# Where three groups of tiles lie in SBUF: the tiles of h 64 bytes apart in their distance from 2 KB, and two gaps in front of the weights and of m

## The chip, the cores and the metric

The kernel runs on one core of a Trainium2 chip. The metric is the device time of one launch, in microseconds (us). Three runs of the kernel before took 1065.42, 1065.43 and 1065.94 us, so the median is 1065.43 us.

## The reference, cut to what matters

The program is two layers of a decoder trunk on 512 tokens of width 1024 and a last RMSNorm. In each layer one wide projection of the normalised input feeds three token mixers (attention, a short convolution, a retention) and their gates; three branch projections are merged and one more projection goes back to the residual stream:

```python
h = rms_norm(x, norm_g)
proj = h @ w_in                       # (512, 1024) @ (1024, 8704)
...
merged = g[:, :, 0] * (branches[0] @ w_branch[0])
for i in range(1, N_BRANCH):
    merged = merged + g[:, :, i] * (branches[i] @ w_branch[i])
return x + (merged @ w_out).astype(x.dtype)
```

Nearly all arithmetic is in `h @ w_in`, `branches[i] @ w_branch[i]` and `merged @ w_out`.

## The kernel before, in words

Everything is laid out with channels on the 128 partitions and the 512 tokens along the free dimension, so one tile of 128x512 float32 takes 2 KB in each partition. Every product is made three times (`mm3`, lines 190 to 193): both operands are split into a high and a low part of type float32r, and line 191 multiplies high by high, line 192 high weights by the low part of the other operand, line 193 low weights by its high part. Each of the three is one matmul with its own load of 128x128 stationary values, which the profile lists as engine PEld.

The weights come as chunks of 128x1024 (4 KB per partition). `split_next` (line 207) copies a chunk's high part to `whi` on ScalarE (line 187) and takes the low part `wlo` on VectorE or GpSimd (line 184); three buffers of each turn. A stationary operand is 128 columns of such a chunk, so it starts at a multiple of 512 bytes from the chunk's start.

In each layer the value projections come first (`values`, line 367: the scaled input `xb` is stationary, the weights are moving). Then h is made, eight tiles with a high and a low part each, so 16 tiles of 2 KB (lines 411 to 417). `proj` (line 420) makes 128 output channels: a loop over k = 0 to 7, `mm3` with h tile k as the moving operand, 24 matmuls in all. There are 60 such projections in a layer. Between k = 3 and k = 4, and after k = 7, `tick` (line 241) may put a step of attention or retention into the stream: score products (line 466), transposes (line 592), value products (lines 191 to 193 on `st` and `vm`), or the two matmuls of a head's norm with the stationary `ones_p` (lines 499 and 500). `merge` (line 621) multiplies branch outputs (moving `xb`) by weights; `out_proj` (line 676) multiplies the merged tiles m (called `vm`, lines 639 to 641, moving) by weights, in the last layer in two halves of 256 tokens.

TensorE's order is written out by hand (line 350); the other engines' order is found by the scheduler when the program is built. Tiles get their addresses when the program is built, pool by pool and name by name in the order in which the names are first used. So all tiles of the large pool before start at the same distance from a multiple of 2 KB, since all sizes but the last are multiples of 2 KB: 384 bytes, for `xb`, `whi`, `wlo`, `qk`, `vm`, `h`, `st` and the rest. The small pool is packed in steps of 32 bytes; `ones_p`, a stationary operand, starts at byte 1440.

Of the kernel before, what the change touches and what calls it, by code (L numbers as in the profile page):

```python
# [18 lines left out]
P = 128  # L19
S = 512  # L20
# [134 lines left out]
def tile_hybrid_trunk(ctx: ExitStack, tc: tile.TileContext, xT, w, prm, lam, tab, cmat, outT):  # L155
# [12 lines left out]
    def t(tag, bufs, shape=(P, S), dt=F32):  # L168
        home = small if tag in SMALL else odd if tag == "wu" else sb
        return home.tile(list(shape), dt, tag=tag, bufs=bufs, name=tag)  # L170

    def tr(tag, bufs, shape=(P, S)):
        return t(tag, bufs, shape, F32R)

    def pj():
        return ps.tile([P, S], F32, tag="pj", bufs=NPJ, name="pj")
# [9 lines left out]
    def split(hi, lo, x, eng=V):  # L186
        A.copy(hi, x)  # L187
        lo_part(lo, x, hi, eng)
# [18 lines left out]
    def split_next():  # L207
        if not raws:
            prefetch()
        if raws:  # L210
            raw = raws.pop(0)
            hi, lo = tr("whi", 3, (P, 1024)), tr("wlo", 3, (P, 1024))
            for c in range(0, 1024, 512):
                c = slice(c, c + 512)
                if pos[0] or parts or c.start:
                    split(hi[:, c], lo[:, c], raw[:, c], G if c.start else V)
                else:
                    V.tensor_copy(hi[:, c], raw[:, c])
                    lo_part(lo[:, c], raw[:, c], hi[:, c])
            parts.append((hi, lo))  # L220
# [53 lines left out]
    nc.sync.dma_start(cm, cmat)  # L274
    ident, negmask, tri = (cm[:, i * P:(i + 1) * P] for i in range(3))
    ones_p = tr("ones_p", 1, (P, P))
    A.copy(ones_p, cm[:, 3 * P:4 * P])
    ones_d = t("ones_d", 1, (P, 1))
# [23 lines left out]

    H = [slice(0, 64), slice(64, 128)]
    klo = [tr("klo", 4) for _ in range(4)]
    for n, lo in enumerate(klo):
        G.memset(lo[H[1 - n % 2]].bitcast(F32), 0.0)
# [44 lines left out]
    for l in range(DEPTH):  # L351
# [59 lines left out]
        h = []  # L411
        for k in range(NK):
            hk = t("wa", 1)
            V.scalar_tensor_tensor(hk, x[k], ng[k], rrow, op0=ALU.mult, op1=ALU.mult)  # L414
            hi, lo = tr("h", 16), tr("h", 16)
            split(hi, lo, hk)
            h.append((hi, lo))
        rv = values_out(rbanks)
# [331 lines left out]
```

## Time and profile before

| | |
|---|---|
| median of three runs | 1065.43 us |
| the profiled execution itself | 1065.34 us |
| its span, first to last instruction | 1063.5 us |
| TensorE busy (PE) | 1053.9 us, 99% of the span |
| weight loads busy (PEld) | 881.7 us |
| VectorE, ScalarE, GpSimd busy | 681.9, 503.0, 318.7 us |
| mean granted TensorE clock | 0.998 of full speed |

The profile's page gives busy times, a picture of the span in slices, and the chain of work that ended last. A matmul's duration in it runs from its start to its modelled end; since matmuls are pipelined, the next one starts before that end, and what one matmul costs is the distance from its start to the next one's start, called spacing below. Starts are read from the timeline.

### The profile page before, as it was taken

The page shows a single profiled execution, that of the slowest core. Times are in us where ns is not written, and L with a number is a line of the kernel's source. Part 1 is how long each engine was busy: PE and PEld are TensorE (multiplying, and loading weights), DVE is VectorE, ACT ScalarE, POOL GpSimd, SP SyncE. Part 2 cuts the span into 40 slices and gives each one's busy share as a digit, 9 for nine tenths or more (in the row PEclk, how much of TensorE's full clock was granted, in tenths as well). Part 3 has the DMA queues.
Part 4 walks back from the last instruction along what each step waited for, and adds up shares of the span by engine and source line. Part 5 has one row for each costly group of instructions (what it writes and reads, how often), then busy time and mean ns, then how long its engine had stood idle before and what let it go on. Part 6 is the DMA issues. An engine that isn't in the chain of part 4 may idle for free.

```text
span 1063.5 us, 13847 instructions
## 1 busy us (share of the span) xinstructions
PE 1053.9 (99%) x5010; PEld 881.7 (83%) x5010; DVE 681.9 (64%) x1168; ACT 503.0 (47%) x943; POOL 318.7 (30%) x253
## 2 busy tenths in 40 slices
PE   9999999999999999999999999999999999999997
PEld 6888888888888888888888888888888888888896
DVE  8687686765677566345528876868556956654444
ACT  6454354543554554334434535445354645543353
POOL 6222232221233333232412212332123233333264
PEclk9999999999999999999999999999999999999999
DMA  6323222232234222444432232223213432133453
GB/s 258 106 93 100 88 71 96 83 119 85 74 119 139 77 85 78 128 129 149 149 99 83 87 109 80 80 84 119 96 60 100 139 100 80 61 107 129 128 190 119
DMA packets 34340, 113.64 MB, mean 107 GB/s; under 512 B 3936, under 2 KB 3936, under 8 KB 34272
## 3 DMA queue, kind: packets, MB, share of 16 engines
q1 hardware_dynamic: 34128, 112.50, 32.4%
q8 instruction: 39, 0.64, 0.3%
q14 instruction: 29, 0.24, 0.1%
q10 hardware_dynamic: 144, 0.26, 0.1%
HBM read 108.55 MB, written 4.19 MB: 106 GB/s over the span
## 4 chain that ended last, share of the span: by engine, by line
PE 93%; DVE 5%; ACT 1%; issue 1%; DMA 0%; SPq 0%; DVEq 0%; ACTq 0%
PE pj L191 28%; PE pj L192 28%; PE pj L193 28%; PE pa L466 3%; PE pa L192 1%; PE pa L193 1%; DVE wa L414 1%; PE pa L191 1%; DVE wlo L184 1%; PE pa L592 1%; DVE h L184 1%; DVE vm L382 1%; ACT h L187 1%; DVE xb L362 0%; PE pa L499 0%
## 5 line engine op out<-in xcount | busy, mean ns | idle before, releaser
L184 POOL TENSOR_TENSOR wlo<-wraw,whi 128x512 fp32r<-128x512 f32 x184 | 251.8, 1371 | 628.0 <-ACT whi L187 582.2
L191 PE MATMUL pj<-h,whi 128*128 128x512 f32 x960 | 379.4, 395 | 0.0
L192 PE MATMUL pj<-h,whi 128*128 128x512 f32 x960 | 374.7, 390 | 0.2
L193 PE MATMUL pj<-h,wlo 128*128 128x512 f32 x960 | 374.7, 390 | 0.0
L187 ACT CAST whi<-wraw 128x512 fp32r<-128x512 f32 x367 | 216.3, 617 | 220.9 <-PE pj L192 141.1
L184 DVE TENSOR_TENSOR wlo<-wraw,whi 128x512 fp32r<-128x512 f32 x184 | 153.1, 833 | 125.5 <-ACT whi L187 124.5
L193 PEld LDWEIGHTS pj<-h,wlo 128*128 128x128 f32 x960 | 180.2, 188 | 38.9 <-DVE wlo L184 0.3
L192 PEld LDWEIGHTS pj<-h,whi 128*128 128x128 f32 x960 | 180.5, 188 | 35.7 <-DVE h L184 1.1
L191 PEld LDWEIGHTS pj<-h,whi 128*128 128x128 f32 x960 | 180.4, 188 | 35.4
L191 PE MATMUL pj<-xb,whi 128*128 128x512 f32 x192 | 75.0, 391 | 0.0
L192 PE MATMUL pj<-xb,whi 128*128 128x512 f32 x192 | 74.9, 390 | 0.0
L193 PE MATMUL pj<-xb,wlo 128*128 128x512 f32 x192 | 74.7, 389 | 0.0
L579 ACT ACTIVATE p<-pa,nm 128x128 f32<-128x128 f32 (+3 forms) x64 | 33.5, 527 | 69.2 <-DVE nm L576 69.0
L503 DVE RECIPROCAL e<-e 128x512 f32<-128x512 f32 x16 | 53.6, 3351 | 18.0 <-ACT e L502 18.0
L187 ACT CAST st<-pa 128x256 fp32r<-128x256 f32 (+2 forms) x80 | 29.8, 373 | 70.5 <-DVE pa L521 40.5
L191 PE MATMUL pj<-vm,whi 128*128 128x256 f32 (+1 forms) x192 | 61.3, 319 | 0.0
L192 PE MATMUL pj<-vm,whi 128*128 128x256 f32 (+1 forms) x192 | 61.1, 318 | 0.0
L193 PE MATMUL pj<-vm,wlo 128*128 128x256 f32 (+1 forms) x192 | 61.1, 318 | 0.0
L636 DVE SCALAR_TENSOR_TENSOR wb<-wa,pj 128x512 f32<-128x512 f32 x32 | 22.0, 687 | 41.5 <-PE pj L193 38.3
L184 DVE TENSOR_TENSOR st<-pa,st 128x256 fp32r<-128x256 f32 (+2 forms) x80 | 33.6, 420 | 17.1 <-ACT st L187 16.5
L193 PEld LDWEIGHTS pj<-xb,wlo 128*128 128x128 f32 x192 | 36.0, 188 | 7.6
L191 PEld LDWEIGHTS pj<-xb,whi 128*128 128x128 f32 x192 | 36.1, 188 | 7.3
(132 smaller groups left out, 1433.6 us busy)
## 6 DMA issues: line engine op xcount, KB each, us to landing
wraw<-w SPq DMA_DIRECT2D x183, 512.0 KB, 3.4
tab<-tab SPq DMA_DIRECT2D x10, 512.0 KB, 3.4
xm<-xT SPq DMA_DIRECT2D x15, 256.0 KB, 3.7
xsave<-xm SPq DMA_DIRECT2D x8, 256.0 KB, 2.0
xm<-xsave SPq DMA_DIRECT2D x8, 256.0 KB, 2.6
outT<-p SPq DMA_DIRECT2D x8, 256.0 KB, 2.1
wraw<-w SPq DMA_DIRECT2D x2, 256.0 KB, 3.4
xm<-xT ACTq DMA_DIRECT2D x1, 256.0 KB, 3.0
```

The costliest lines, as they stand in the source:

```text
L184: eng.tensor_tensor(lo, x, hi, op=ALU.subtract)
L187: A.copy(hi, x)
L191: T.matmul(out, wh, xh, start=start, stop=False)
L192: T.matmul(out, wh, xl, start=False, stop=False)
L193: T.matmul(out, wl, xh, start=False, stop=stop)
L382: V.scalar_tensor_tensor(lo, banks[tt], rtok[:, tt:tt + 1], hi, op0=ALU.mult, op1=ALU.subtract)
L414: V.scalar_tensor_tensor(hk, x[k], ng[k], rrow, op0=ALU.mult, op1=ALU.mult)
L466: T.matmul(o, ac[i][:, asl], bc[i][:, bsl], start=i == 0, stop=i == 1)
L503: V.reciprocal(r, r)
L579: A.activation(pc[:, :n], sp[:, :n], AF.Exp, bias=nm, scale=0.125, accum_out=sm)
L592: T.transpose(tp[:, j * P:(j + 1) * P], p1[:, j * P:(j + 1) * P], ident)
L636: V.scalar_tensor_tensor(y, g, 1.0, o, op0=ALU.add, op1=ALU.mult)
```

## The change

The tag `h` with 16 rotating buffers becomes 16 tags `h0` to `h15` with one buffer each, high and low part of tile k being h(2k) and h(2k + 1). Each is allocated with 16 float32 more than are used, so 2112 bytes instead of 2048. A tile of 256 bytes per partition that nothing uses is allocated just before the first `whi`, one of 128 bytes just before the first `vm`.

```diff
     def tr(tag, bufs, shape=(P, S)):
+        if tag == "whi" and "gap0" not in gaps:
+            gaps["gap0"] = t("gap0", 1, (P, 64))
+        if tag == "vm" and "gap1" not in gaps:
+            gaps["gap1"] = t("gap1", 1, (P, 32))
         return t(tag, bufs, shape, F32R)
+
+    gaps = {}
...
-            hi, lo = tr("h", 16), tr("h", 16)
+
+            hi, lo = (tr(f"h{2 * k + i}", 1, (P, S + 16))[:, 0:S] for i in range(2))
             split(hi, lo, hk)
```

The built programs have the same instructions on all five engines in the same order, with the same waits; only names and addresses differ. The distance of a tile's start from a multiple of 2 KB, in bytes:

| tiles | before | after |
|---|---|---|
| `xm`, `wa`, `cm`, `klo`, `xb` | 384 | 384 |
| `whi`, `wlo`, `qk`, `e1`, `e2` | 384 | 640 |
| `vm` (values, later m) | 384 | 768 |
| `h`, by number n = 0 to 15 | 384 | 768 + 64 n |
| `tab`, `ez`, `p0`, `p1`, `st`, `sq`, `wc`, `wu` | 384 | 1792 |
| `ones_p` (small pool) | 1440 | 1440 |

## Rows read from the trace of the kernel before

**Rows 1.** The page: span, busy times, slices of PE and its clock, chain by engine.
```profile
span 1063.5 us, 13847 instructions
PE 1053.9 (99%) x5010; PEld 881.7 (83%) x5010; DVE 681.9 (64%) x1168; ACT 503.0 (47%) x943; POOL 318.7 (30%) x253
...
PEclk9999999999999999999999999999999999999999
...
PE 93%; DVE 5%; ACT 1%; issue 1%; DMA 0%; SPq 0%; DVEq 0%; ACTq 0%
```

**Rows 2.** Busy time by stretch: 100 to 1000 us (busy, count; PEclk, DMA share, GB/s).
```profile
100.00:1000.00 900.00, 899.88 (x4151) 749.12 (x4150) 575.02 (x992) 421.44 (x789) 253.34 (x192) 1.00 0.31 100
```

**Rows 3.** Matmuls grouped by line and shape: count, busy us, mean ns, idle before.
```profile
L191 PE MATMUL pj<-h,whi 128*128 128x512 f32 x960 | 379.4, 395 | 0.0
L192 PE MATMUL pj<-h,whi 128*128 128x512 f32 x960 | 374.7, 390 | 0.2
L193 PE MATMUL pj<-h,wlo 128*128 128x512 f32 x960 | 374.7, 390 | 0.0
L191 PE MATMUL pj<-xb,whi 128*128 128x512 f32 x192 | 75.0, 391 | 0.0
...
L191 PE MATMUL pj<-vm,whi 128*128 128x256 f32 x128 | 36.4, 284 | 0.0
...
L191 PE MATMUL pj<-whi,xb 128*128 128x512 f32 x64 | 25.5, 399 | 0.0
...
L191 PE MATMUL pa<-whi,xb 128*128 128x512 f32 x64 | 25.3, 396 | 0.0
...
L191 PE MATMUL pj<-vm,whi 128*128 128x512 f32 x64 | 24.9, 389 | 0.0
```

**Rows 4.** Timeline of TensorE, seven undisturbed projections (start us, duration us).
```profile
179.77 0.39 PE L191 MATMUL pj<-h,whi 128*128 128x512 f32 x1
...
217.85 0.22 PE L466 MATMUL pa<-qk 128*128 128x128 f32 x1
```

**Rows 5.** Timeline of TensorE, output projection with 256 columns, last layer.
```profile
1049.40 0.28 PE L191 MATMUL pj<-vm,whi 128*128 128x256 f32 x1
...
1053.72 0.28 PE L191 MATMUL pj<-vm,whi 128*128 128x256 f32 x1
```

**Rows 6.** Timeline of TensorE around a head's norm (lines 499, 500).
```profile
137.28 0.39 PE L192 MATMUL pj<-h,whi 128*128 128x512 f32 x1
...
138.18 0.40 PE L193 MATMUL pj<-h,wlo 128*128 128x512 f32 x1
138.42 0.39 PE L499 MATMUL pa<-st,ones_p 128*128 128x512 f32 x1
138.65 0.39 PE L500 MATMUL pa<-st,ones_p 128*128 128x512 f32 x1
138.88 0.40 PE L191 MATMUL pj<-h,whi 128*128 128x512 f32 x1
...
140.96 0.39 PE L191 MATMUL pj<-h,whi 128*128 128x512 f32 x1
141.18 0.39 PE L192 MATMUL pj<-h,whi 128*128 128x512 f32 x1
```

**Rows 7.** Timeline of TensorE, first score products of 256 columns after a projection.
```profile
130.91 0.28 PE L466 MATMUL pa<-qk 128*128 128x256 f32 x1
131.02 0.28 PE L466 MATMUL pa<-klo,qk 128*128 128x256 f32 x1
131.14 0.28 PE L466 MATMUL pa<-qk 128*128 128x256 f32 x1
```

## The prediction

> **What bounds the kernel.** I read the page first, then the busy times of the long middle stretch, then the groups of matmuls, and last the timeline of TensorE alone. The page [rows 1] shows TensorE busy for 1053.9 of 1063.5 us and 93% of the chain that ended last on it; its granted clock stands at the upper of its two levels (2.4 GHz) throughout. Between 100 and 1000 us it is idle for 0.12 us of 900, while VectorE is busy for 575 us, ScalarE for 421 and GpSimd for 253 [rows 2]. So only two things could move the time: how far apart the matmuls start, or another engine that gets so much slower that TensorE waits for it.
>
> The timeline gives the spacing. In seven projections in a row, 168 matmuls of 512 columns start between 179.77 and 217.85 us: 38.08 us / 168 = 226.7 ns each [rows 4]. With 256 columns, 36 matmuls take 4.32 us, 120.0 ns each [rows 5]. The difference, 106.7 ns for 256 columns, is 0.417 ns per column, one cycle of 2.4 GHz. So 512 columns themselves take 213.3 ns, and 13.3 ns come on top of every matmul, of either length. That fixed part is what a move of addresses can touch. Each matmul's moving read runs beside the load of the next matmul's stationary values, so the two reads may hinder each other, and then it matters where the two operands lie.
>
> **The change part by part.** No instruction, wait or DMA is added, removed or moved; no queue is passed. Three things differ, and they have one answer together: the start of the weights, of m and of h relative to each other. Before, moving and stationary operands all start 384 bytes past a multiple of 512, since a slice of a chunk is a multiple of 512 bytes. After, the weights stand at 128 past such a multiple, h tile n at 256 + 64 n, xb still at 384, m and the values at 256. The matmuls whose pair of operands changes are, by the counts [rows 3]: 3 x 960 = 2880 of h, 3 x 192 = 576 of the merges, 3 x (64 + 64) = 384 of the value projections and 3 x 64 = 192 of the first output projection, 4032 with 512 columns; and 3 x 128 = 384 of the last output projection with 256. The attention's value products keep their pair (st and vm both at 256 past 512).
>
> The trace has no matmul with such a pair, so I bound its spacing from both sides.
>
> Below: the fixed part cannot go under nothing, 13.3 ns less for each of 4416 matmuls, 58.7 us, or 1006 us.
>
> Above: the widest spacing at an odd address is that before a head's norm. The matmul at 138.18 us starts its successor 0.24 us later, while the projection before it kept 0.2267: about 8 ns more [rows 6]. What loads during it is `ones_p`, the only large stationary operand that does not start at a multiple of 64 bytes (1440 is 22.5 x 64). 8 ns on 4416 matmuls are 35 us, or 1101 us.
>
> Between these ends I take the row that is nearest in kind, the long run [rows 4]. The addresses in it differ in everything from 512 bytes upward: eight slices of a chunk, six weight buffers, 16 tiles of h over 32 KB. The spacing is 226.7 ns all the same, so address bits from 512 bytes up do nothing. The head's norm says that a step of 32 bytes does something. The change moves starts by 64, 128 and 256 bytes, just between. What decides for me is the time that the pace after a disturbance needs: from 138.18 to 140.96 us there are 12 matmuls in 2.78 us where 12 x 226.7 ns make 2.72 [rows 6], then the old pace is back; the delay is about 0.05 us, and the pace falls back to the same 226.7 ns whatever operands follow. A spacing that always comes back to the same value looks like reads that repeat their pattern within a short stretch of addresses. At 0.417 ns and 4 bytes per column, 64 bytes pass in 6.7 ns, half the fixed part. If the pattern repeats after 64 bytes, every start in the changed kernel, all multiples of 64, is equal to every start before, and only `ones_p` stands out, as it does. So I put the term at 0 for all 4416 matmuls, with the ends above kept for the range.
>
> The other engines read and write the same tiles at moved addresses. Their prices are the rows of before; were each of their 512-column operations 5% slower, VectorE's 575 us in 900 would be 604, still beside TensorE, so I cost that at nothing. It would count only where VectorE itself is on the chain, 5% of 1063.5 us or 53 us [rows 1]; 5% of that is 2.7 us, which I keep for the range.
>
> The sum is the profiled execution's own 1065.34 us + 0, which is 0.09 us under the median of the runs.
>
> On the independence of reads, the trace was weighed against the Trainium skill. [...] TensorE: Matmul & The Clock Gate, section "What happens when you issue a matmul", adds that loading the next weights takes no bandwidth from the running matmul, and gives 215.7 ns for 512 columns. The trace does not agree with that last figure: 226.7 ns here, with a load beside every matmul. If the missing 11 ns are a conflict of two reads and the change removed it everywhere, 4032 x 11 ns = 44 us, or 1021 us.
>
> **The rivals.** First rival, faster: the weight load and the moving read meet because both start at the same place, and a different place spares one step of the conflict. For it speaks a row: the first score product after a projection keeps 0.11 us to its successor, the next 0.12 [rows 7]; so a pair with less than the whole fixed part exists, about 6.7 ns less at 256 columns. Against it: there the load's size and the neighbours differ, not the place. Price: of the 16 tiles of h two (n = 6 and 14, both high parts, 2 x 2 x 120 = 480 matmuls) keep the old pair, so 2400 x 6.7 ns = 16 us from h alone, 1049 us; with merges, values and output projections (576 + 384 + 192 + 384 = 1536 more) 26 us, 1039 us. I put this case at 1045.
>
> Second rival, slower: the even pace of 226.7 ns is itself a state that a constant distance of the operands makes possible. After the disturbance at 138.88 us nine matmuls take 2.08 us, 231 ns each, before the pace is even again [rows 6]. With h stepping 64 bytes between high and low part and 128 from k to k + 1, the distance changes at every matmul of a projection, and the pace could stay in that disturbed state. Place: the 2880 matmuls of h. Price: 2880 x 4.5 ns = 13 us, 1078 us. It decides from some 470 matmuls on (470 x 4.5 ns = 2.1 us). For it: the disturbance costs the same whatever follows, so it is a matter of phase, and phase is what the change keeps moving. Against it: projections and merges follow each other, with quite different tiles, without any disturbance.
>
> That the change does not do what it says is part of the forecast: it moves the starts as told, but by multiples of 64 bytes that the reads may not tell apart.
>
> **How the numbers follow.** Forecast (no effect): 0.48, 1065.3 us, its own range 1063.5 to 1067. Faster: 0.32, from 1037 to 1062. Slower: 0.20, from 1068 to 1085. The range from 1043 to 1077 leaves out some 0.09 of the lower case and 0.08 of the upper. A change under 0.2% (2.1 us) can hardly be told from none; a small part of the forecast's weight goes to either side, and back from the rivals' near ends, so the chances stay 0.32, 0.48 and 0.20.
>
> **What would show it.** The timeline of a quiet projection is the whole test: 24 matmuls in 5.44 us if I am right, 5.28 (220 ns) for the first rival, 5.5 or more with spacings that do not settle for the second. If h stays at 226.7 while merges or output projections move, the staggering was idle and the gaps acted. Idle time of TensorE in 100 to 1000 us should stay near 0.1 us. The prediction is wrong if a quiet projection's spacing changes by more than 1 ns, since 4032 matmuls make 4 us of it.

## The result, and the profile after

The changed kernel takes 1077.45 us (median of 4 runs, 1077.04 to 1077.67) against 1065.43 us: the ratio is 1.0112 with a 95% interval of 1.0094 to 1.0129. It is slower by 12 us. The forecast was no effect at 1065.3 us; the upper end of the range was 1077.

The page of the changed kernel answers to [rows 1] (same columns):

```profile
span 1075.6 us, 13847 instructions
PE 1065.5 (99%) x5010; PEld 881.1 (82%) x5010; DVE 681.0 (63%) x1168; ACT 503.0 (47%) x943; POOL 318.6 (30%) x253
...
PEclk9999999999999999999999999999999999999998
...
PE 97%; DVE 1%; ACT 0%; DMA 0%; issue 0%; SPq 0%; DVEq 0%; ACTq 0%
```

TensorE's busy time grew by 11.6 us (1053.9 to 1065.5) and the span by 12.1; the other engines are as busy as before, and the granted clock is at TensorE's upper level in both. So the loss is hardly waiting: the matmuls themselves stand further apart. The stretch from 100 to 1000 us says it in one number, against [rows 2]:

```profile
100.00:1000.00 900.00, 899.97 (x4103) 740.14 (x4102) 570.40 (x985) 416.47 (x780) 250.49 (x190) 1.00 0.30 98
```

TensorE is idle for 0.03 us of 900 (0.12 before), with a granted clock of 1.00 in both, but starts 4103 matmuls in that time instead of 4151.

The timeline of TensorE, seven quiet projections in a row (start us, duration us), answers to [rows 4]. `mm3` is now at lines 197 to 199:

```profile
181.79 0.39 PE L197 MATMUL pj<-h,whi 128*128 128x512 f32 x1
...
220.61 0.23 PE L473 MATMUL pa<-qk 128*128 128x128 f32 x1
```

The same 168 matmuls take 38.82 us instead of 38.08: 231.1 ns each instead of 226.7. Their spacing also never becomes even; within one of these projections some matmuls keep 0.23 us to the next and some 0.24:

```profile
187.33 0.39 PE L197 MATMUL pj<-h,whi 128*128 128x512 f32 x1
187.56 0.39 PE L198 MATMUL pj<-h,whi 128*128 128x512 f32 x1
187.80 0.39 PE L199 MATMUL pj<-h,wlo 128*128 128x512 f32 x1
188.03 0.39 PE L197 MATMUL pj<-h,whi 128*128 128x512 f32 x1
...
188.72 0.39 PE L197 MATMUL pj<-h,whi 128*128 128x512 f32 x1
```

And the output projection of layer 0, where all tiles of m lie alike:

```profile
491.19 0.40 PE L197 MATMUL pj<-vm,whi 128*128 128x512 f32 x1
...
535.98 0.39 PE L197 MATMUL pj<-whi,xb 128*128 128x512 f32 x1
```

192 matmuls in 44.79 us are 233.3 ns each. That already speaks against the mechanism of my second rival, since the distance of m from the weights is the same, 128 bytes, at every one of them. Adding up the spacings from the starts of all matmuls, the h projections take 671.5 us instead of 662.1 (+9.4), that output projection 1.3 more, the merges 0.7 and the value projections 0.5: 11.9 of the 12 us. The last two are not paid by their own pairs of operands. Of the twelve matmuls of a merge the slower ones are among the first seven, behind an h projection; the last five keep 227 ns as before. And the value projections' 0.5 us is one wait near the start: the matmul at 22.75 us is followed only after 1.15 us, its counterpart before after 0.53.

### The profile page after: what moved, and what is told of

Same layout as the page of the kernel before. It is cut to its first block, busy times and chain, and to the rows that moved or that the text cites. A ratio compares the mean times of both kernels' runs of the same rounds, so it can differ in the third digit from the quotient of the medians.

```text
span 1075.6 us, 13847 instructions
## 1 busy us (share of the span) xinstructions
PE 1065.5 (99%) x5010; PEld 881.1 (82%) x5010; DVE 681.0 (63%) x1168; ACT 503.0 (47%) x943; POOL 318.6 (30%) x253
## 4 chain that ended last, share of the span: by engine, by line
PE 97%; DVE 1%; ACT 0%; DMA 0%; issue 0%; SPq 0%; DVEq 0%; ACTq 0%
PE pj L199 29%; PE pj L197 29%; PE pj L198 29%; PE pa L473 3%; PE pa L199 2%; PE pa L198 2%; PE pa L197 2%; PE pa L599 1%; DMA xm<-xT 0%; DVE xb L368 0%; PE pa L506 0%; PE pa L507 0%; DVE e L333 0%; DVE p L715 0%; PE pa L341 0%
## 5 line engine op out<-in xcount | busy, mean ns | idle before, releaser
L199 PE MATMUL pj<-h,wlo 128*128 128x512 f32 x960 | 378.6, 394 | 0.0
L193 ACT CAST whi<-wraw 128x512 fp32r<-128x512 f32 x367 | 216.3, 617 | 231.4 <-PE pj L198 146.4
```

Source lines behind the costliest of these rows:

```text
L199: T.matmul(out, wl, xh, start=False, stop=stop)
```

## The experiments

Three theories stood against each other. "Distance": the spacing depends on how far the stationary operand starts from the moving one, whether that changes or not. "Constancy", my second rival: any constant distance settles at 226.7 ns, and only change from matmul to matmul costs. "Own start": a moving tile that starts at some place is slower by itself. No experiment changes the arithmetic; only names, lengths and places of tiles differ. Distances below are the start of the stationary operand minus that of the moving one, modulo 512 bytes; that of m in the changed kernel is -128, which is 384.

**e1_gaps_only.** The gaps of the change, h as before:

```diff
-            hi, lo = (tr(f"h{2 * k + i}", 1, (P, S + 16))[:, 0:S] for i in range(2))
+            hi, lo = tr("h", 16), tr("h", 16)
```

> Both gaps, h left as 16 buffers of one tag: weights start 128 past a multiple of 512 bytes, h and m at 256, all of h alike. Theory 'distance' (the spacing is set by the distance of the moving start from the start of the stationary operand that loads beside it, whether it changes or not): h gets the pace that m has in the changed kernel, 233.3 ns instead of 226.7, so 2880 x 6.7 = 19 us and 1.3 us for m, about 1085 us, slower than the changed kernel. Theory 'constancy' (my second rival: any constant distance settles at 226.7 ns, only change from matmul to matmul costs): 1066 +- 2 us. Theory 'own start' (a moving tile that starts elsewhere than 384 past 512 bytes is slower by itself): 1085 us as well.

Measured: 1080.95 us, ratio 1.0141 (1.0125 to 1.0158), slower than the change as a whole. Four quiet projections, 96 matmuls:

```profile
58.61 0.40 PE L197 MATMUL pj<-h,whi 128*128 128x512 f32 x1
...
81.01 0.40 PE L197 MATMUL pj<-h,whi 128*128 128x512 f32 x1
```

22.40 us are 233.3 ns each, at one constant distance (-128). "Constancy" falls. The time is 4 us under the 1085 that I expected: the price per matmul was taken against the quiet pace, but some matmuls behind an inserted attention or retention step ran at about 231 ns before too [rows 6], and had less to lose. By the starts, the 62 of 120 projections with an inserted step gained 3.5 ns per matmul, the other 58 gained 5.8.

**e2_stagger_only.** h staggered, no gaps:

```diff
-            hi, lo = tr("h", 16), tr("h", 16)
+            hi, lo = (tr(f"h{2 * k + i}", 1, (P, S + 16))[:, 0:S] for i in range(2))
```

> h staggered by 64 bytes, no gaps: weights and m at 384 past 512 bytes as before. All theories: the h projections keep their mean of about 231 ns (distance and start run through the same eight values, and change at every matmul): 1065.4 + 10 = 1075.5 +- 1.5 us; the output projection of layer 0 is back at 226.7 ns by 'distance' and by 'own start'.

Measured: 1077.14 us, ratio 1.0107 (1.0092 to 1.0122), just over the upper end of what was expected. The first two rows are the seven quiet projections, the last two the output projection of layer 0:

```profile
181.61 0.40 PE L191 MATMUL pj<-h,whi 128*128 128x512 f32 x1
...
220.44 0.22 PE L466 MATMUL pa<-qk 128*128 128x128 f32 x1
...
491.64 0.39 PE L191 MATMUL pj<-vm,whi 128*128 128x512 f32 x1
...
535.16 0.39 PE L191 MATMUL pj<-whi,xb 128*128 128x512 f32 x1
```

h has 38.83 us / 168 = 231.1 ns, as in the changed kernel; m is back at 43.52 us / 192 = 226.7 ns. So the stagger alone makes the whole loss of h, and the gaps alone make one of their own; together they don't add up, because both only choose distances.

**e3_weights_gap_only.** The gap in front of the weights alone, which moves everything allocated behind it as well:

```diff
+        if tag == "whi" and "g_whi" not in gaps:
+            gaps["g_whi"] = t("g_whi", 1, (P, 64))
```

> Only the gap of 256 bytes in front of the weights: weights, h and m all start 128 past 512 bytes, xb stays at 384, so the distance is 0 for h and m and 256 for the merges. 'Distance': 1065.4 +- 1 us, h at 226.7 ns. 'Constancy': the same. 'Own start': h starts at another place and costs like m in the changed kernel, 5 us or more slower, 1071 to 1085 us.

Measured: 1065.64 us, ratio 1.0000 (0.9990 to 1.0009). The seven quiet projections:

```profile
179.98 0.39 PE L195 MATMUL pj<-h,whi 128*128 128x512 f32 x1
...
218.06 0.22 PE L470 MATMUL pa<-qk 128*128 128x128 f32 x1
```

38.08 us, 226.7 ns, though h starts 256 bytes further than before. A start 256 bytes further is not slower by itself, and a distance of 256, which the merges have here, costs nothing. "Own start" is not settled by this run alone, since it may repeat after 256 bytes; e4 settles it for the moving tile.

**e4_scan_0_64_192.** Every weight buffer gets its own name and length, so that the three stand at three distances and the projections take turns:

```diff
-            hi, lo = tr("whi", 3, (P, 1024)), tr("wlo", 3, (P, 1024))
+            hi, lo = weights("whi", turn[0] % 3), weights("wlo", turn[0] % 3)
+            turn[0] += 1
...
+    turn = [0]
+
+    def weights(x, n):
+        return tr(f"{x}{'abc'[n]}", 1, (P, 1024 + (16, 32, 80)[n]))[:, 0:1024]
+
+    for x in ("whi", "wlo"):
+        for n in range(3):
+            weights(x, n)
```

> h, xb and m at one start; the three weight buffers of each kind stand 0, 64 and 192 bytes further (mod 512), so that projections take turns in three constant distances. 'Distance': projections with distance 0 run at 226.7 ns, those with 64 and 192 each at a mean of their own, between 229 and 236 ns. 'Constancy': all three settle at 226.7 ns within some ten matmuls of a projection's start. 'Own start': all at 226.7 ns throughout.

The first matmuls of projections in a row, with the buffers' names (a at 0, b at 64, c at 192), and the matmuls around the step from a to b:

```profile
58.02 0.39 PE L191 MATMUL pj<-h,whia 128*128 128x512 f32 x1
...
63.23 0.39 PE L193 MATMUL pj<-h,wloa 128*128 128x512 f32 x1
63.46 0.40 PE L191 MATMUL pj<-h,whib 128*128 128x512 f32 x1
63.70 0.39 PE L192 MATMUL pj<-h,whib 128*128 128x512 f32 x1
...
69.06 0.40 PE L191 MATMUL pj<-h,whic 128*128 128x512 f32 x1
...
74.57 0.40 PE L191 MATMUL pj<-h,whia 128*128 128x512 f32 x1
```

24 matmuls take 5.44 us at 0 (226.7 ns), 5.60 at 64 (233.3) and 5.51 at 192 (229.6, with some matmuls at its start that have not settled). The kernel took 1083.84 us in its one run. "Distance" holds as expected, and 64 and 192 bytes are not mirror images. "Own start" of the moving tile falls here: h stays where it was, and its pace changes with the weights. At the step from a to b the matmul at 63.23 us, beside which the first weights of b load, keeps its pace (226 ns, from the starts in ns); the one at 63.46 us, the first to use them, takes 236.

One rule remains that no run excludes: that each operand's own start counts, repeating after 256 bytes, for no run moves both operands of the 512-column projections together by less than that. The nearest rows speak for the distance: in e1 the value products of the retention have both operands (`st` and `vm`) 128 bytes further modulo 256 than before, and the first two of three matmuls of 512 columns take 231 and 227 ns (medians of eight), much like the 229 and 228 of e4, where this pair is not moved.

**e5_low_part_256.** The distance is 256 at the second of the three lines of `mm3` and 0 at the other two:

```diff
-            hi, lo = tr("h", 16), tr("h", 16)
+            hi = tr("hx", 8)
+            if k == 0 and l == 0:
+                t("gap0", 1, (P, 64))
+            lo = tr("hy", 8)
```

> The eight high tiles of h stay 384 past 512 bytes, the eight low tiles stand 256 further, so the distance of moving and stationary start changes between 0 and 256 at every line of a projection. 'Distance' (0 and 256 cost alike, as the merges of the run with the weights' gap show): h at 226.7 ns, 1065.7 +- 1 us. 'Constancy' (a distance that changes from matmul to matmul keeps the pace from settling): h near 231 ns, 1078 us.

Measured: 1065.79 us, ratio 1.0000 (0.9991 to 1.0009).

```profile
180.09 0.39 PE L191 MATMUL pj<-hx,whi 128*128 128x512 f32 x1
...
218.17 0.22 PE L469 MATMUL pa<-qk 128*128 128x128 f32 x1
```

Again 38.08 us for 168. A distance that changes between 0 and 256 costs nothing. Since 0 and 256 turn out alike below (e7), this says again that 256 is free; what a change between distances that differ modulo 256 costs, it doesn't tell.

**e6_scan_32_96_160** and **e7_scan_320_384_448** are e4 with other lengths of the weight buffers and, where the first distance isn't 0, a tile in front of them.

> Three weight buffers of each kind at 32, 96 and 160 bytes from h, xb and m (mod 512). 'Distance' in steps of 32 bytes: each has a settled mean of its own; from ones_p (32 bytes off) I expect 229 to 235 ns for 32, and 229 to 236 for 96 and 160. A distance with less than 226.7 ns would be a way to a faster kernel. If only steps of 64 counted: 32 like 0 (226.7), 96 like 64 (233.3), 160 like 128 (233.3).

> Three weight buffers of each kind at 320, 384 and 448 bytes from h, xb and m (mod 512). If the pattern repeats after 256 bytes: 320 like 64 (233.3 ns), 384 like 128 (233.3), 448 like 192 (229). If it repeats after 512 only: 384 at 233.3 (as with both gaps alone, distance -128), the other two unlike 64 and 192.

The first matmuls of projections in a row in e6 (a at 32, b at 96, c at 160):

```profile
58.40 0.40 PE L191 MATMUL pj<-h,whia 128*128 128x512 f32 x1
...
64.00 0.39 PE L191 MATMUL pj<-h,whib 128*128 128x512 f32 x1
...
69.62 0.39 PE L191 MATMUL pj<-h,whic 128*128 128x512 f32 x1
...
75.22 0.40 PE L191 MATMUL pj<-h,whia 128*128 128x512 f32 x1
```

and in e7 (c at 448, a at 320, b at 384; the last row is the score product behind that projection):

```profile
69.37 0.40 PE L191 MATMUL pj<-h,whic 128*128 128x512 f32 x1
...
74.88 0.39 PE L191 MATMUL pj<-h,whia 128*128 128x512 f32 x1
...
80.47 0.39 PE L191 MATMUL pj<-h,whib 128*128 128x512 f32 x1
...
86.05 0.22 PE L477 MATMUL pa<-qk 128*128 128x128 f32 x1
```

e6: 5.60, 5.62 and 5.60 us, so 233.3, 234.2 and 233.3 ns; steps of 32 count. e7: 5.51 us at 448 (229.6 ns), 5.59 at 320 (232.9), 5.58 at 384 (232.5). That is 192 and 64 of e4 and the 128 of e1 over again, within 1 ns: together with e3, the pattern repeats after 256 bytes at all four distances compared. The two kernels took 1095.53 and 1088.95 us in one run each.

**e8_ones_at_384.** The experiments pointed to a small gain, since `ones_p` is the one large operand with a distance other than 0 (32) in the kernel before. Out of the small pool it lands at 384 past 512, and all other tiles keep their distances:

```diff
-    SMALL = ("par", "eps", "lam_e", "ones_p", "ones_d", "nlam0", "nlam1", "gsub0", "gsub1", "rtok", "nm", "sm")
+    SMALL = ("par", "eps", "lam_e", "ones_d", "nlam0", "nlam1", "gsub0", "gsub1", "rtok", "nm", "sm")
```

> Only the stationary ones_p moves, from 416 to 384 past 512 bytes, where all other operands start. 'Distance': the 235, 231 and 229 ns around a head's norm become 226.7, and the nine disturbed matmuls behind them as well: 16 norms x 0.053 us = 0.85 us, 1064.8 us. 'Own start' or a cost of the norm itself (its wait, its bank): no change, 1065.7 us.

Measured: 1064.86 us against 1065.60, ratio 0.9992 with an interval of 0.9983 to 1.0001: as large as expected, but its interval reaches no change. The timeline around a head's norm is clear, against [rows 6]:

```profile
139.26 0.39 PE L193 MATMUL pj<-h,wlo 128*128 128x512 f32 x1
139.49 0.39 PE L499 MATMUL pa<-st,ones_p 128*128 128x512 f32 x1
139.71 0.39 PE L500 MATMUL pa<-st,ones_p 128*128 128x512 f32 x1
139.94 0.39 PE L191 MATMUL pj<-h,whi 128*128 128x512 f32 x1
...
141.30 0.39 PE L191 MATMUL pj<-h,whi 128*128 128x512 f32 x1
```

Nine matmuls from 139.26 take 2.04 us, 226.7 ns each; there is no disturbance left. This version has the lowest median of all that ran, by a difference within its interval.

**e9_scan_16_224_240**, e4 once more, with buffers whose used part begins 16 bytes into the tile where needed:

> Three weight buffers of each kind at 16, 224 and 240 bytes from h, xb and m (mod 512). What is asked: is 0 the best distance, or only the best among multiples of 32? 'Distance' with a repeat of 256: 224 is -32, 240 is -16; 32 gave 233 ns and 192 gave 229, so I expect 224 between 227 and 234, 16 and 240 between 226.7 and 233. Anything below 226.7 ns as a settled mean would make a faster kernel. If steps under 32 bytes did not count, 16 would run at 226.7 ns.

```profile
58.41 0.40 PE L191 MATMUL pj<-h,whia 128*128 128x512 f32 x1
...
64.00 0.39 PE L191 MATMUL pj<-h,whib 128*128 128x512 f32 x1
...
69.59 0.40 PE L191 MATMUL pj<-h,whic 128*128 128x512 f32 x1
...
75.06 0.39 PE L191 MATMUL pj<-h,whia 128*128 128x512 f32 x1
...
80.50 0.39 PE L191 MATMUL pj<-h,whib 128*128 128x512 f32 x1
```

224 (b) takes 5.59 us, 232.9 ns. 240 (c) takes 5.47 us, 227.9, and its later matmuls run at 226.7, as in 13 of the 19 projections without an inserted step at this distance. 16 (a) takes 5.59 us the first time and 5.44, or 226.7 ns, the second: the same operands at the same distance run at two paces. What differs is what ran before: of the 16 projections at this distance without an inserted step, the eleven that keep 226.7 to 227.4 in their second half all follow an even pace, and four of the five at 232.6 to 233.5 an uneven one. No distance tried settled under 226.7 ns at 512 columns, so there the kernel before had the best one, and this scan (1083.77 us in one run) gave no faster kernel.

**e10_low_weights_64.** Only the low weights stand 64 bytes further:

```diff
-            hi, lo = tr("whi", 3, (P, 1024)), tr("wlo", 3, (P, 1024))
+            hi = tr("whi", 3, (P, 1024))
+            if not pos[0] and not parts:
+                t("gap0", 1, (P, 16))
+            lo = tr("wlo", 3, (P, 1024))
+            if not pos[0] and not parts:
+                t("gap1", 1, (P, 112))
```

> Only the low weights stand 64 bytes further than everything else. In a projection the second of three matmuls (high weights, low part of h) runs while low weights load, the third uses them while high weights load. 'Distance, of the load beside the running matmul': the second line is slow, the other two stay near 226.7 ns. 'Distance, of the operand in use': the third line is slow. Either way the three together take 2 x 226.7 + about 233.3 = 687 ns or some more, against 680 before: 960 x 7 ns = 6 to 7 us, about 1072 us.

```profile
63.75 0.39 PE L191 MATMUL pj<-h,whi 128*128 128x512 f32 x1
63.98 0.39 PE L192 MATMUL pj<-h,whi 128*128 128x512 f32 x1
64.20 0.40 PE L193 MATMUL pj<-h,wlo 128*128 128x512 f32 x1
64.44 0.39 PE L191 MATMUL pj<-h,whi 128*128 128x512 f32 x1
64.67 0.39 PE L192 MATMUL pj<-h,whi 128*128 128x512 f32 x1
64.90 0.40 PE L193 MATMUL pj<-h,wlo 128*128 128x512 f32 x1
65.13 0.39 PE L191 MATMUL pj<-h,whi 128*128 128x512 f32 x1
```

One third of the matmuls has a distance of 64, yet six take 1.38 us, 230 ns each, and the mean over 192 matmuls of m at the same pattern, from their starts, is 231.1 ns: 693 ns for three, 13 more than before and not 7. The one run took 1077.56 us where I had about 1072, so I missed the size. The third line is the slow one (236 ns as the mean of its starts), which uses the low weights while high ones load; that reads as "the operand in use", as the step from a to b in e4 does. But the matmul ahead of a head's norm is slow while `ones_p`, at 32, only loads [rows 6]. Which of the two loads meets the read is not settled.

The last output projection, with 256 columns, goes the other way:

```profile
1055.73 0.28 PE L191 MATMUL pj<-vm,whi 128*128 128x256 f32 x1
...
1059.97 0.28 PE L191 MATMUL pj<-vm,whi 128*128 128x256 f32 x1
```

36 matmuls take 4.24 us, 117.8 ns each, where the kernel before has 120.0 [rows 5]. So a distance of 0 throughout, best at 512 columns, is not best at 256.

## Why the prediction was wrong

Right was the frame. TensorE's spacing was the only thing to look at; no other engine became the bound, and VectorE's allowance of 2.7 us was not needed. The starts moved as listed. Not all 4416 pairs changed in a way that counts, though: of the 2880 of h, the 480 at n = 6 and 14 keep their distance, which the first rival says and the list does not, and the 480 at n = 2 and 10 as well as the 960 of merges and value projections stand 256 apart, which is free (e3). The test named for it, a quiet projection's 24 matmuls against 5.44 us, gave the answer: 38.82 us / 7 = 5.55 us.

The step that failed is "If the pattern repeats after 64 bytes, every start in the changed kernel, all multiples of 64, is equal to every start before." The pattern repeats after 256 bytes (e7, e3), and within 256 bytes distances of 32, 64, 96, 128, 160, 192 and 224 all cost (e1, e4, e6, e9): the term put at 0 measured 4.4 ns for each matmul of a quiet h projection and 6.6 ns for each of the first output projection. The rows had only told that multiples of 512 are alike and that 32 is not; everything between was open, and I closed the gap by an argument on how long 64 bytes take at 0.417 ns a column. That was a guess about a period from one time, without a row at any of the distances in question. The head's norm [rows 6] was also read too narrowly: that the disturbance behind the norm always ran back to the same pace showed only that operands behind it were at distance 0, where the pace is good.

The bound from above, 8 ns per matmul from [rows 6], was sound: the distances that cost at 512 columns took 2.9 to 7.5 ns over 226.7 (1.2 at 240).

The second rival gave 1078 us for a result of 1077.45, at the right place, for a reason that is only half right; that the total agrees to 1 us is in part luck, for its 13 us were all to come from h. Its price of 4.5 ns per matmul of h is what the quiet projections show (231.1 - 226.7 = 4.4). Its mechanism, that any constant distance settles at 226.7 ns and only change costs, is refuted: at a constant 128 bytes the loss is larger (e1). What is left of it: mixed distances cost somewhat more than the mean of their settled paces. The stagger runs through 128, 64, 0 and 192 modulo 256; with the high parts counted twice these settle at about 230.3 ns in the mean (229.8 for the high parts, 231.4 for the low ones), and it runs at 231.1; in e10 the extra was about 2 ns. Why there are several settled paces (233 and 227 ns at 16 bytes), and what in the memory repeats after 256 bytes, no run here shows; nor, as said at e4, does one exclude that each operand's own start counts.

The price came out as 9.4 us for h and not 12.7 (2880 x 4.4 ns) because the h projections of the kernel before were not at 226.7 ns throughout: behind each inserted step some matmuls already ran at about 231 ns. The rest came from the output projection of layer 0, the starts of the merges and one wait in the value projections.

The first rival, faster, fell at 512 columns. The rows taken for it, 0.11 us once after a projection [rows 7], show operands at distance 0, as all products of the kernel before, so they never spoke of another place; and none of the distances tried settled under 226.7 ns. At 256 columns it has a grain of truth, 117.8 ns against 120.0 in e10, but the changed kernel had only 0.4 us from that.

The Trainium skill's SBUF — State Buffer, section "SBUF: two separate sides", says that on the engine side only the port pair that VectorE and GpSimd share causes contention, and that TensorE never waits on anyone. Here that does not tell the whole: with the same instructions in the same order and nothing but addresses moved, the kernel takes 1065.72 us or 1080.95 (e1).

## What to carry to other kernels

Where TensorE runs float32r matmuls back to back and every one has its own weight load, look up where the moving and the stationary tiles start: in this kernel equal starts modulo 256 bytes were the best of all tried for 512 columns, and a spread that looks like it avoids collisions cost 1%. A pad or a small constant tile in the wrong place can disturb the pace unseen, as `ones_p` did around every head's norm. At 256 columns the order was another, so look at the shape that takes the time. When the rows leave a stretch of distances untested, forecast from both ends of it and don't let a tidy period decide.

## What the runs showed of the hardware that was not expected

- The spacing of 512-column float32r matmuls, each with a load of its own, by distance modulo 256 bytes, from quiet projections: 226.7 ns at 0; 233.3 at 32; 233.3 at 64; 234.2 at 96; 232.5 to 233.3 at 128; 233.3 at 160; 229.6 at 192; 232.9 at 224; 227.9, later 226.7, at 240; 226.7 or 232.9 at 16. Over all projections without an inserted step in the four scans, 16 to 23 at each distance, the means of the second twelve matmuls lie within 0.7 ns of these values, and at 228.9 for 16 bytes.
- At 256 columns a distance of 128 cost nothing: adding up starts, the last output projection of the changed kernel took 0.4 us less than before, and with the low weights at 64 (e10) 36 of its matmuls took 4.24 us instead of 4.32.
- A pace can hold through a whole projection of 24 matmuls and still be one of two for the same distance: at 16 bytes 5.59 us behind a disturbed projection, 5.44 behind an even one (e9).
